# A PSUM bank moved, a merge step delayed and the samples' turns given their own steps, in the attention of a four-layer trunk

## The chip, the core and the metric

The kernel runs on one core of a Trainium2 chip. The metric is the device time of one execution in microseconds (us). A core has a matrix engine, TensorE (PE in the profile; its weight loads are PEld), which reads on-chip SBUF and writes the accumulator memory PSUM; three engines for elementwise work, VectorE (DVE), ScalarE (ACT) and GpSimd (POOL); and SyncE (SP), which here only issues DMA transfers. Each engine runs its own instructions in the order in which they were written, and waits on semaphores for the others. PSUM has eight banks. A bank that holds a result can be written again only when its readers are done.

## The reference, cut to what matters

A prompt of 1024 positions and 8 single-token samples go through an attention layer, a ConvGLU, a pooling layer and another ConvGLU. Only the attention is touched here. It has three groups of 16 heads, with dilations 1, 4 and 16; each query reads at most the 129 keys s-128..s of its own residue stream, and a bias table is added to the logits.

```python
    s = jnp.einsum("nbqhd,nbkhd->nbhqk", qb, kb).astype(jnp.float32) * SCALE
    s = s + bias[:, np.clip(rel, 0, SPAN)]
    s = jnp.where(valid[None, :, None], s, NEG_INF)
    m = jnp.max(s, axis=-1)
    p = jnp.exp(s - m[..., None])
    l = jnp.sum(p, axis=-1)
    o = jnp.einsum("nbhqk,nbkhd->nbqhd", p.astype(v.dtype), vb).astype(jnp.float32)
...
    w = l * jnp.exp(m - jnp.max(m, axis=0))
    w = w / jnp.sum(w, axis=0)
    return jnp.einsum("gbthd,gbth->bthd", o, w)
```

The last three lines merge the three groups per head. The samples do the same against caches of keys and values.

## The kernel before, in words

**Units.** The attention is cut into 24 units: eight pairs of heads (`hp`), each with the groups g = 2, 1, 0 in this order. For each unit TensorE makes q, k and v: nine groups of 24 matmuls (line 125; each float32 product is three fast products of high and low halves). While it does this for one unit, the attention of the unit before is fed in between the matmuls. A unit takes some 48 us.

**The order.** It is written by a plan, not by the hardware. `attend` lays down steps with a place on a clock that counts one for every three matmuls; a unit has 72 of them. For block i of 128 queries, `scores` stands at place 6i+1, the transposition of the softmax weights (`probs_t`, tile `pt`) at 6i+15 and the value sums (`pv`, tile `o`) at 6i+24; the transpositions of v (`transpose_v`, tile `vt`) stand at 4 and 28. `between()` runs what has come due. Two queues of small tasks hang on the same clock: `extra` takes one task at 4, 10, 16, ... and `behind` one at 7, 13, 19, .... What a task returns is put on `urgent`, of which one step is run after each three matmuls, ahead of the plan. What is left at the end of a unit is flushed.

**Packing.** The queries and keys of the next unit are split into high and low halves late in a unit: `pack_q` (lines 402 to 404) and `pack_k` (lines 413 to 415), between places 29 and 59, on DVE, ACT and POOL.

**Banks.** Matmuls of q, k, v have two banks (`mm`). The attention has six: three for `o`, one each for `pt`, `s` and `misc`. `misc` is shared by the transposed values `vt`, the merge's transposition `mt`, and all that the samples do: `qr`, `ssc`, `selfp`, the samples' value products `spv` (line 773) and their turned sums `spt` (line 796).

**Merge.** After g = 0 of a pair, `Merge` queues in `extra`: two pauses, `weights` (DVE lines 574 to 582, one exponential on ACT), `rows` (TensorE transposes the weights into `mt`, line 587; DVE copies them out, line 589; they go to DRAM), and then for each group a `fetch` of the weights spread over partitions and an `apply`, which multiplies and adds on POOL (lines 607 and 609), then `store`. With the places above, `weights` falls at place 64 and `rows` at 70 of a unit, the fetches and applies in the next unit.

**Samples.** Every odd pair also carries two heads' pairs of the samples (`Sample`, four in all, `pc` 0 to 3). Their value part, `values`, runs through twelve products; after each third one the sum is turned (`turn`: two tiny matmuls per head into `spt`, then two DVE adds, line 800).

Of the kernel before, what the change touches and what calls it, by code (L numbers as in the profile page):

```python
# [11 lines left out]
F32 = mybir.dt.float32  # L12
# [18 lines left out]
TAB = 384  # L31
# [16 lines left out]
def trunk(ctx: ExitStack, tc: tile.TileContext, a, out):  # L48
# [135 lines left out]
    class Norm:  # L184
        def __init__(self, x, gain, c, place, engines):


            self.engines = engines
            self.lows = [nc.vector] if gain == 3 else ([nc.vector, nc.gpsimd] * 2 + [nc.vector] * 4)[:8 if gain + c == 0 else 2]
            self.x, self.gain, self.c, self.place = x, gain, c, place  # L190
            self.c0, self.c1 = CHUNKS[c]
            self.w = self.c1 - self.c0
            self.blocks = sub_blocks(self.w)
            self.done, self.rows, self.acc, self.squares, self.pending = False, {}, [], 0, None
# [92 lines left out]
    with ExitStack() as ph:  # L287
        qp = ph.enter_context(tc.tile_pool(name="qkv", bufs=1))
        mmp = ph.enter_context(tc.tile_pool(name="mmp", bufs=1, space=PSUM))
        app = ph.enter_context(tc.tile_pool(name="app", bufs=1, space=PSUM))  # L290
# [8 lines left out]
        def load_x(c):  # L299
            c0, c1 = CHUNKS[c]  # L300
            for k in range(8):
                nc.sync.dma_start(out=xT[k][:, c0:c1], in_=a["x"][:, k, c0:c1])

        def place(kind, j=0, c=0):
            if kind in ("row", "square"):
                return qp.tile([128, 512], F32, name="nrow", tag="p", bufs=4)
            if kind == "acc":
                return part[:, j, CHUNKS[c][0]:CHUNKS[c][1]]
            if kind == "vec":
                return qp.tile([128, 4, 4], F32, name="nv", tag="nv", bufs=2)  # L310
            banks.rotate(1)
            return app.tile([128, 512], F32, name="nstat", tag=banks[0], bufs=3 if banks[0] == "o" else 1)

        nc.scalar.activation(warm, ones, AF.Sqrt)
        banks = deque(["o", "o", "pt", "misc", "o", "s"])
        load_x(0)
        w_load(0)
        nc.sync.dma_start(out=consts, in_=a["consts"])
# [14 lines left out]
        def tables():  # L333

            def step(g, tag, src):
                ps = app.tile([16, TAB], F32, name="btp", tag=tag)
                ps = ps[:, :src.stop - src.start]
                nc.tensor.matmul(ps, rb[:, 16 * g:16 * g + 16], onehots[g][:, src], start=True, stop=True)
                if src.start == 0:
                    nc.vector.scalar_tensor_tensor(masks[g], ps, -1.0, masks[g], op0=ALU.mult, op1=ALU.subtract)  # L340
                    nc.sync.dma_start(out=bias_tab[:, g], in_=masks[g])
                else:
                    bs = qp.tile([16, 512], F32, name="bs", tag="p", bufs=4)[:, :136]
                    nc.vector.tensor_copy(bs, ps)
                    nc.sync.dma_start(out=bias_smp[:, g], in_=bs)

            return [partial(step, g, *x) for g in (2, 1, 0) for x in (("s", slice(0, TAB)), ("pt", slice(TAB, TAB + 136)))]

        norms = [Norm(lambda k: xT[k], 0, c, place, (nc.vector, nc.gpsimd)) for c in range(3)]

        def squares(c):
# [74 lines left out]
        def has_prev(g, i):  # L426
            return (g == 0 and i > 0) or (g == 1 and i % 2 == 1)
# [47 lines left out]

        def probs_t(u, j):
            w = 256 if j < 7 and has_prev(u.g, j + 1) else 128
            ps = app.tile([128, 2, 256], F32, name="pt", tag="pt")
            for h in range(2):
                nc.tensor.transpose(ps[:, h, 0:128], u.p[j][:, h, 0:128], ident)  # L480
                if w == 256:
                    nc.tensor.transpose(ps[:, h, 128:256], u.p[j + 1][:, h, 128:256], ident)
            phl = qp.tile([128, 2, 2, 256], F32R, name="phl", tag="phl", bufs=2)
            nc.scalar.activation(phl[:, :, 0, :w], ps[:, :, :w], AF.Copy)  # L484
            nc.vector.tensor_sub(phl[:, :, 1, :w], ps[:, :, :w], phl[:, :, 0, :w].bitcast(F32))  # L485
            u.pt[j] = (phl, w)

        def pv_mm(u, j, b0, b1, first):


            q = (j + b0) % 2
            for h in range(2):
                for x in range(2):
                    nc.tensor.matmul(u.o[:, h, 128 * q:128 * (q + b1 - b0)], u.v[j // 4][:, j % 4, h, :],
                                     u.pt[j][0][:, h, x, 128 * b0:128 * b1], start=first and h + x == 0, stop=True,
                                     skip_group_check=True)

        def pv(u, j):
            first = j % 2 == 0
            if first:  # L500
                u.o = app.tile([128, 2, 256], F32, name="o", tag="o", bufs=3)
                if j and u.pt[j - 1][1] == 256:
                    pv_mm(u, j - 1, 1, 2, True)
                    first = False
            pv_mm(u, j, 0, 1 if j % 2 else u.pt[j][1] // 128, first)
            if j % 2:

                x = 256 * (j // 2 % 2)
                tmp = (part[:, 0, x:x + 256] if (u.hp, u.g) != order[23] else
                       qp.tile([128, 256], F32, name="ot", tag="ot", bufs=1))  # L510
                u.tmp = tmp, u.o
                for h, (own, other) in enumerate(((A, B), (B, A))):
                    nc.scalar.activation(tmp[own], u.o[other, h], AF.Copy)
# [35 lines left out]
        class Merge:  # L549
            def __init__(self, hp):  # L550
                self.hp, self.us = hp, [units[hp, g] for g in range(3)]
                self.st, self.cb = units[hp, 0].others, {}
                pause = lambda: None
                if hp < 7:
                    extra.extend([pause, pause, self.weights, self.rows])
                else:
                    self.weights()
                    extra.extend([pause, self.rows])
                if hp < 7:
                    extra.extend([lambda: self.fetch(2), pause, lambda: self.apply(2),  # L560
                                  lambda: self.fetch(1), lambda: self.apply(1),
                                  lambda: self.fetch(0), lambda: self.apply(0), pause, self.store])
                else:
                    extra.extend([lambda: [self.fetch(g) for g in (2, 1, 0)] and None, pause, lambda: self.apply(2),
                                  lambda: self.apply(1), lambda: self.apply(0), self.store])
# [56 lines left out]
        class Sample:  # L622
# [7 lines left out]
            def group(self, g):  # L630
# [21 lines left out]
                if g == 0:  # L652
# [11 lines left out]
                    for i in range(self.pc < 3, 13 + len(self.rooms)):  # L664
                        behind.append(lambda i=i: self.values(i))

            def cols(self, cache, g, b, n):
                row = cache[g][b][:, 256 * self.pc:256 * self.pc + 256]
                w = (128, 512, 2048)[g]
                return bass.AP(tensor=row.tensor, offset=row.offset,  # L670
                               ap=[[8 * w, 128], [1024 * w, n], [1, 256]])
# [81 lines left out]
            def values(self, n):  # L753


                todo = []
                m = n - len(self.rooms)
                if 0 <= m < 12:
                    i, g = divmod(m, 3)
                    if not g and i:  # L760
                        todo.append(partial(self.turn, i - 1, self.sum))
                    todo.append(partial(self.products, i, g, self.rooms[m % len(self.rooms)]))
                if m == 12:
                    todo.append(partial(self.turn, 3, self.sum))
                if n < 12:
                    todo.append(partial(self.fetch, n))
                return todo
# [34 lines left out]
        extra, behind = deque(), deque()  # L802
# [103 lines left out]
        for n, (hp, g) in enumerate(order):  # L906
            u = units[hp, g] = Unit()
# [8 lines left out]
            for i, (which, c) in enumerate(seq):  # L916
# [12 lines left out]
                ps = mmp.tile([128, 352], F32, name="mm", tag="mm", bufs=2)  # L929
# [58 lines left out]
        for n, ct in enumerate(OUT):  # L988
# [9 lines left out]
            for c in range(3):  # L998
                c0, c1 = CHUNKS[c]
                ps = mmp.tile([128, 352], F32, name="mm", tag="mm", bufs=2)  # L1000
# [51 lines left out]
    def norm(gain, c, *engines):  # L1052
        return Norm(lambda k: xT[k], gain, c, place, engines)
# [363 lines left out]
```

## Time and profile before

| what | us |
|---|---|
| median of 3 runs | 2878.77 (2878.76 to 2883.21) |
| the profiled execution | 2875.72 |
| its span, first to last instruction | 2873.9 |
| PE busy in the span | 2777.4 (97%) |
| DVE / ACT / POOL busy | 1629.4 / 1361.1 / 1074.2 |

The span is read in stretches. From 85 to 1160 us the units of the pairs 0 to 6 and most of 7 run; until 85 us the first norms and loads, from 1160 to 1400 us the end of the attention, the output projection and the first norms of the next layer; after that the ConvGLUs and the pooling layer. A matmul's row in the profile lasts about twice as long as the distance to the next one, since they are pipelined: "busy" hides part of a wait, and what counts is when the next one starts.

### The profile page before, as it was taken

The page shows a single profiled execution, that of the slowest core. Times are in us where ns is not written, and L with a number is a line of the kernel's source. Part 1 is how long each engine was busy: PE and PEld are TensorE (multiplying, and loading weights), DVE is VectorE, ACT ScalarE, POOL GpSimd, SP SyncE. Part 2 cuts the span into 40 slices and gives each one's busy share as a digit, 9 for nine tenths or more (in the row PEclk, how much of TensorE's full clock was granted, in tenths as well). Part 3 has the DMA queues.
Part 4 walks back from the last instruction along what each step waited for, and adds up shares of the span by engine and source line. Part 5 has one row for each costly group of instructions (what it writes and reads, how often), then busy time and mean ns, then how long its engine had stood idle before and what let it go on. Part 6 is the DMA issues. An engine that isn't in the chain of part 4 may idle for free. (4 is left out here: it accounts for less than half of the span.)

```text
span 2873.9 us, 46685 instructions
## 1 busy us (share of the span) xinstructions
PE 2777.4 (97%) x18109; PEld 2736.4 (95%) x18109; DVE 1629.4 (57%) x3330; ACT 1361.1 (47%) x2748; POOL 1074.2 (37%) x865
## 2 busy tenths in 40 slices
PE   6999999999999999999999999999999999999998
PEld 5999999999999998899999999999999999999998
DVE  6666656665666566755333234687755334346655
ACT  5565665566556665634223223445542233334443
POOL 4335453545354535445444434111133343331110
PEclk9999999999999999999999999999999999999999
DMA  3234332433243333537222222333422226223543
GB/s 115 61 76 135 85 98 74 124 96 96 79 120 99 93 81 108 169 111 99 74 67 74 67 74 74 110 118 118 135 88 67 74 67 76 73 68 116 173 143 92
DMA packets 203949, 277.80 MB, mean 97 GB/s; under 512 B 70272, under 2 KB 154096, under 8 KB 203728
## 3 DMA queue, kind: packets, MB, share of 16 engines
q1 hardware_dynamic: 203680, 274.80, 34.8%
q8 instruction: 142, 2.33, 0.3%
q14 instruction: 79, 0.65, 0.1%
q10 hardware_dynamic: 48, 0.02, 0.0%
HBM read 251.89 MB, written 23.34 MB: 96 GB/s over the span
## 5 line engine op out<-in xcount | busy, mean ns | idle before, releaser
L125 PE MATMUL mm<-hh,w_hi 128*128 128x352 f32 (+2 forms) x4064 | 1340.5, 330 | 9.3 <-ACT hh L256 3.3
L125 PE MATMUL mm<-hl,w_hi 128*128 128x352 f32 (+2 forms) x4064 | 1305.3, 321 | 5.0 <-DVE hl L260 5.0
L125 PE MATMUL mm<-hh,w_lo 128*128 128x352 f32 (+2 forms) x4064 | 1305.2, 321 | 1.8 <-DVE w_lo L105 1.8
L125 PEld LDWEIGHTS mm<-hh,w_hi 128*128 128x128 f32 x4064 | 769.8, 189 | 15.7 <-ACT hh L256 3.8
L125 PEld LDWEIGHTS mm<-hl,w_hi 128*128 128x128 f32 x4064 | 770.5, 190 | 7.1 <-DVE hl L260 6.5
L125 PEld LDWEIGHTS mm<-hh,w_lo 128*128 128x128 f32 x4064 | 768.9, 189 | 2.6 <-DVE w_lo L105 2.6
L105 POOL TENSOR_TENSOR w_lo<-w_raw,w_hi 128x1024 fp32r<-128x1024 f32 x212 | 514.0, 2425 | 574.2 <-ACT w_hi L104 561.3
L104 ACT ACTIVATE w_hi<-w_raw 128x1024 fp32r<-128x1024 f32 x348 | 364.7, 1050 | 290.7 <-PE mm L125 266.0
L1119 DVE SCALAR_TENSOR_TENSOR conv<-gate,convp,conv 128x336 f32<-128x336 f32 (+1 forms) x176 | 220.5, 1253 | 384.9 <-ACT conv L1117 375.9
L125 PE MATMUL mm<-gh,w_hi 128*128 128x352 f32 (+2 forms) x1056 | 340.5, 322 | 4.0 <-ACT gh L1110 2.1
L125 PE MATMUL mm<-gh,w_lo 128*128 128x352 f32 (+2 forms) x1056 | 339.9, 322 | 1.9 <-DVE w_lo L105 1.9
L125 PE MATMUL mm<-gl,w_hi 128*128 128x352 f32 (+2 forms) x1056 | 339.8, 322 | 0.3 <-POOL gl L1111 0.3
L1057 DVE TENSOR_TENSOR x<-x,mm 128x352 f32<-128x352 f32 (+2 forms) x312 | 157.1, 510 | 225.8 <-PE mm L125 225.3
L472 ACT ACTIVATE p<-p,st 128x128 f32<-128x128 f32 (+1 forms) x384 | 169.9, 443 | 201.4 <-DVE st L469 200.7
L1111 POOL TENSOR_TENSOR gl<-conv,gh 128x352 fp32r<-128x352 f32 (+2 forms) x132 | 123.5, 937 | 339.1 <-ACT gh L1110 336.1
L105 DVE TENSOR_TENSOR w_lo<-w_raw,w_hi 128x1024 fp32r<-128x1024 f32 x136 | 166.7, 1226 | 87.6 <-ACT w_hi L104 87.5
L125 PEld LDWEIGHTS mm<-gh,w_hi 128*128 128x128 f32 x1056 | 199.8, 189 | 4.6 <-ACT gh L1110 2.4
L125 PEld LDWEIGHTS mm<-gh,w_lo 128*128 128x128 f32 x1056 | 200.1, 190 | 2.2 <-DVE w_lo L105 2.2
L125 PEld LDWEIGHTS mm<-gl,w_hi 128*128 128x128 f32 x1056 | 199.9, 189 | 0.7 <-POOL gl L1111 0.7
L485 DVE TENSOR_TENSOR phl<-pt,phl 128x512 fp32r<-128x512 f32 (+1 forms) x192 | 104.7, 545 | 167.0 <-ACT phl L484 165.9
L373 ACT ACTIVATE raw<-mm 128x336 f32<-128x336 f32 (+1 forms) x216 | 144.5, 670 | 99.1 <-PE mm L125 96.7
L1102 ACT ACTIVATE gate<-mm 128x352 f32<-128x352 f32 (+2 forms) x132 | 60.2, 457 | 262.1 <-PE mm L125 262.1
(190 smaller groups left out, 3118.6 us busy)
## 6 DMA issues: line engine op xcount, KB each, us to landing
w_raw<-in_w_in SPq DMA_DIRECT2D x176, 512.0 KB
w_raw<-in_w_out SPq DMA_DIRECT2D x88, 512.0 KB
w_raw<-in_w_qkv SPq DMA_DIRECT2D x72, 512.0 KB
x<-qd SPq DMA_DIRECT2D x48, 256.0 KB
kc<-in_cache_k SPq DMA_DIRECT2D x48, 256.0 KB
vc<-in_cache_v SPq DMA_DIRECT2D x48, 256.0 KB
x<-c_d SPq DMA_DIRECT2D x42, 256.0 KB
out_new_k<-raw SPq DMA_DIRECT2D x8, 516.0 KB
```

What stands on the lines that cost most here:

```text
L104: nc.scalar.activation(hi, raw, AF.Copy)
L105: (eng or (nc.vector if i in quick else nc.gpsimd)).tensor_sub(lo, raw, hi.bitcast(F32))
L125: nc.tensor.matmul(ps, l, r, start=first and i == 0, stop=last and i == n - 1)
L373: nc.scalar.activation(stream(raw[:, :T], u.g, c0, t1, which > 0), ps[:, :w].rearrange("p (s r) -> p s r", r=DILS[u.g]), AF.Copy, scale=si ...
L472: nc.scalar.activation(p[:, h, :w], p[:, h, :w], AF.Exp, bias=u.st[:, i, h, 0:1], scale=-1.0, accum_out=u.st[:, i, h, 1:2])
L485: nc.vector.tensor_sub(phl[:, :, 1, :w], ps[:, :, :w], phl[:, :, 0, :w].bitcast(F32))
L1057: nc.vector.tensor_add(xT[ct][:, c0:c1], xT[ct][:, c0:c1], ps)
L1102: nc.scalar.activation(gate[:, 2 + s:2 + e], group(tiles8(w, c), c), AF.Copy)
L1111: nc.gpsimd.tensor_sub(self.gl[f][:, s:e], conv[:, s:e], self.gh[f][:, s:e].bitcast(F32))
L1119: nc.vector.scalar_tensor_tensor(conv[:, :n], gate[:, j:j + n], cw[j], conv[:, :n], op0=ALU.mult, op1=ALU.add)
```

## The change: what it does

Three edits. One of the three banks of `o` becomes a second bank of `pt` (the norms' and the bias table's temporary tiles follow suit). In the merges of the pairs 0 to 6 a pause is put between `weights` and `rows`: `rows` and all that follows in the merge come one `extra` place (six clock places) later. For the samples 0 to 2 `turn` is no longer returned by `values` along with a product, but is a task of its own in `behind`, so that the later products each come one to four places later; sample 3 stays as it was.

```diff
             banks.rotate(1)
-            return app.tile([128, 512], F32, name="nstat", tag=banks[0], bufs=3 if banks[0] == "o" else 1)
+            return app.tile([128, 512], F32, name="nstat", tag=banks[0], bufs=2 if banks[0] in ("o", "pt") else 1)
...
-        banks = deque(["o", "o", "pt", "misc", "o", "s"])
+        banks = deque(["o", "o", "pt", "misc", "pt", "s"])
...
-                ps = app.tile([16, TAB], F32, name="btp", tag=tag)
+                ps = app.tile([16, TAB], F32, name="btp", tag=tag, bufs=2 if tag == "pt" else 1)
...
-            ps = app.tile([128, 2, 256], F32, name="pt", tag="pt")
+            ps = app.tile([128, 2, 256], F32, name="pt", tag="pt", bufs=2)
...
-                u.o = app.tile([128, 2, 256], F32, name="o", tag="o", bufs=3)
+                u.o = app.tile([128, 2, 256], F32, name="o", tag="o", bufs=2)
...
                 if hp < 7:
-                    extra.extend([pause, pause, self.weights, self.rows])
+                    extra.extend([pause, pause, self.weights, pause, self.rows])
...
                     for i in range(self.pc < 3, 13 + len(self.rooms)):
                         behind.append(lambda i=i: self.values(i))
 
+                        if self.pc < 3 and i and i % 3 == 0:
+                            behind.append(lambda i=i: self.turn(i // 3 - 1, self.sum))
+
...
-                    if not g and i:
+                    if not g and i and self.pc == 3:
                         todo.append(partial(self.turn, i - 1, self.sum))
                     todo.append(partial(self.products, i, g, self.rooms[m % len(self.rooms)]))
-                if m == 12:
+                if m == 12 and self.pc == 3:
                     todo.append(partial(self.turn, 3, self.sum))
```

TensorE's order at the start of the unit after the merge of pair 0, as a difference (`mt` is the merge's transposition, `vt` the transposed values; both live in the one bank `misc`):

```order
 L125 MATMUL mm<-hh,w_lo 128x352
 L445 MATMUL vt<-consts,raw 128x128 x4
+L587 MATMUL mt<-consts,me 48x128
 L125 MATMUL mm<-hh,w_hi 128x352
 L125 MATMUL mm<-hl,w_hi 128x352
```

`mt` stood three matmuls ahead of the unit's end and now stands right behind the four transpositions into `vt`, with no matmul between them. The same holds at all seven merges of the pairs 0 to 6.

TensorE's order at the first turn of sample 0, as a difference (`spt` is the turned sum, `spv` the samples' product; both in `misc`):

```order
-L125 MATMUL mm<-hh,w_lo 128x336
-L796 MATMUL spt<-selm,spv_sb 128x4 x2
-L125 MATMUL mm<-hh,w_hi 128x336
-L125 MATMUL mm<-hl,w_hi 128x336
-L125 MATMUL mm<-hh,w_lo 128x336
-L773 MATMUL spv<-x_3561,pst 16x256 x4
+L799 MATMUL spt<-selm,spv_sb 128x4 x2
+L125 MATMUL mm<-hh,w_hi 128x336
+L125 MATMUL mm<-hl,w_hi 128x336
+L125 MATMUL mm<-hh,w_lo 128x336
```

Three matmuls stood between the turned sum and the next product in the same bank; now the product comes a whole `behind` place later. (Line numbers behind the new lines are three higher.)

GpSimd's order in the second unit after the merge of pair 0, before:

```order
L105 TENSOR_TENSOR w_lo<-w_raw,w_hi 128x1024
L607 TENSOR_TENSOR x_1403<-x_1403,x_2369 128x1024
L609 TENSOR_TENSOR x_916<-x_916,x_1403 128x1024
L404 TENSOR_TENSOR x_593<-raw,x_593 64x512
L650 TENSOR_TENSOR kc<-kc,x_2377 128x512
L607 TENSOR_TENSOR x_1913<-x_1913,x_2488 128x1024
L609 TENSOR_TENSOR x_916<-x_916,x_1913 128x1024
L650 TENSOR_TENSOR kc<-kc,x_2377 128x512
L404 TENSOR_TENSOR x_593<-raw,x_593 64x512
L105 TENSOR_TENSOR w_lo<-w_raw,w_hi 128x1024
L650 TENSOR_TENSOR kc<-kc,x_2377 128x512
L415 TENSOR_TENSOR k_100<-raw,k_100 64x512
```

and after (607 and 609 are the merge's multiply and add, 404 and 415 pack queries and keys, 650 multiplies the samples' keys, 105 splits weights):

```order
L105 TENSOR_TENSOR w_lo<-w_raw,w_hi 128x1024
L404 TENSOR_TENSOR x_593<-raw,x_593 64x512
L607 TENSOR_TENSOR x_1403<-x_1403,x_2430 128x1024
L609 TENSOR_TENSOR x_916<-x_916,x_1403 128x1024
L650 TENSOR_TENSOR kc<-kc,x_2374 128x512 x2
L404 TENSOR_TENSOR x_593<-raw,x_593 64x512
L607 TENSOR_TENSOR x_1913<-x_1913,x_2532 128x1024
L609 TENSOR_TENSOR x_916<-x_916,x_1913 128x1024
L105 TENSOR_TENSOR w_lo<-w_raw,w_hi 128x1024
L650 TENSOR_TENSOR kc<-kc,x_2374 128x512
L415 TENSOR_TENSOR k_100<-raw,k_100 64x512
```

The last multiply and add of the merge stood ahead of the second part of the queries; now they stand behind it, where the keys are packed.

## Rows read from the trace of the kernel before

**Rows 1.** Windows: stretch and length; each engine's busy us; PE clock; DMA.
```profile
85.00:1160.00 1075.00, 1038.79 (x7143) 1016.12 (x7142) 693.05 (x1802) 643.06 (x1629) 483.20 (x285) 1.00 0.36 97
```
**Rows 2.** Waits of PE, 85 to 1160 us: total us, times, longest.
```profile
PE pt L480 <- DVE phl L485: 11.7, 15, 1.7
PE o L494 <- DVE phl L485: 9.2, 9, 1.9
PE mt L587 <- DVE me L582: 8.7, 4, 2.2
PE spv L773 <- DVE so L800: 5.4, 6, 1.3
PE spt L796 <- DVE ct L589: 1.0, 3, 0.3
```
**Rows 3.** Timeline at an odd pair's merge: start, us, instruction [idle before, releaser].
```profile
347.98 0.91 PE L773 MATMUL spv<-x,pst 128*16 128x256 f32 x4 [1.26 <-DVE so L800]
...
359.84 0.60 PE L796 MATMUL spt<-selm,spv_sb 16*128 16x4 f32 x4 [0.32 <-DVE ct L589]
361.00 0.62 PE L773 MATMUL spv<-x,pst 128*16 128x256 f32 x4 [0.55 <-DVE so L800]
...
364.47 0.41 PE L125 MATMUL mm<-hh,w_hi 128*128 128x352 f32 x1
365.38 0.69 DVE L449 TENSOR_TENSOR vhl<-vt,vhl 128x512 fp32r<-128x512 f32 x1 [1.55 <-ACT vhl L448]
```
**Rows 4.** Windows of 3.3 us around two of the samples' waits.
```profile
348.20:351.50 3.30, 3.30 (x15) 3.12 (x13) 1.97 (x4) 1.26 (x2) 2.09 (x3) 0.50 0.68 236
352.00:355.30 3.30, 3.30 (x25) 3.17 (x25) 2.42 (x7) 1.74 (x3) 0.38 (x1) 1.00 0.23 67
...
928.50:931.80 3.30, 3.30 (x15) 3.17 (x14) 1.98 (x4) 1.26 (x2) 2.16 (x3) 0.50 0.70 234
```
**Rows 5.** Timeline at an even pair's merge and into the next unit.
```profile
201.36 0.44 PE L480 MATMUL pt<-consts,p 128*128 128x128 f32 x2 [0.48 <-DVE phl L485]
...
207.54 0.55 PE L494 MATMUL o<-phl,vhl 128*128 128x128 f32 x3 [0.58 <-DVE phl L485]
...
212.21 0.29 PE L587 MATMUL mt<-consts,me 128*48 128x128 f32 x1 [2.18 <-DVE me L582]
212.72 0.85 DVE L530 TENSOR_TENSOR x<-o,part 64x256 f32<-64x256 f32 x2
213.60 0.28 DVE L589 COPY ct<-mt 48x128 f32<-48x128 f32 x1
214.11 1.06 ACT L104 ACTIVATE w_hi<-w_raw 128x1024 fp32r<-128x1024 f32 x1
215.82 0.40 PE L125 MATMUL mm<-hh,w_hi 128*128 128x352 f32 x1
216.73 0.69 DVE L449 TENSOR_TENSOR vhl<-vt,vhl 128x512 fp32r<-128x512 f32 x1 [1.55 <-ACT vhl L448]
```
**Rows 6.** Timeline of PE, DVE and POOL in that next unit, packing stage.
```profile
237.57 0.44 PE L480 MATMUL pt<-consts,p 128*128 128x128 f32 x2 [0.84 <-DVE phl L485]
...
241.78 2.41 POOL L607 TENSOR_TENSOR x<-x,x 128x1024 f32<-128x1024 f32 x1 [3.58 <-DMA x<-c_d]
244.27 2.51 POOL L609 TENSOR_TENSOR x<-x,x 128x1024 f32<-128x1024 f32 x1
244.51 2.82 DVE L404 TENSOR_TENSOR x<-raw,x 64x512 fp32r<-64x512 f32 x1
249.16 0.44 PE L480 MATMUL pt<-consts,p 128*128 128x128 f32 x2 [0.57 <-DVE phl L485]
256.21 0.55 PE L494 MATMUL o<-phl,vhl 128*128 128x128 f32 x3 [1.91 <-DVE phl L485]
```
**Rows 7.** One line's durations, 85 to 1160 us: ns min/median/max, start, form.
```profile
L404 DVE TENSOR_TENSOR x<-raw,x x45: 686/687/2894, 97.5 to 1152.5; 64x512 fp32r<-64x512 f32 x45
L607 POOL TENSOR_TENSOR x<-x,x x21: 2382/2395/2412, 220.5 to 1111.3; 128x1024 f32<-128x1024 f32 x21
```

## The prediction

> **What bounds the kernel now.** First the windows by stage: between 85 and 1160 us, where the change lies, TensorE shows 1038.8 of 1075 us busy at the full clock, so about 36 us of idle time is all that three edits to the order of the attention can remove there [rows 1]. DVE is busy 693 us in the same stretch: on average it is far from full. Then TensorE's waits in this stretch [rows 2]. They add up to 36.0 us, and every one of them ends with a DVE instruction. That is the thing to see: the three edits aim at four of the five rows (pt, mt, spv, spt: 26.8 us), but what is late each time is DVE. Where DVE is late because its own queue is full, a wait that is taken away from one place comes back at the next thing that TensorE needs from DVE. So I read the timeline at each wait and asked whether DVE stands idle soon after it (then the wait is really saved) or works without a pause until the next wait (then it is given back).
>
> **The samples' turns.** The turned sum and the next product share the bank misc, with three matmuls between them; now a whole place lies between. The six spv waits (5.4 us) and the three spt waits behind the merge's copy (1.0 us) go, and DVE has idle time there: it waits 1.55 us for ACT at 365 us [rows 2, 3]. That is -6.4 us. The long one of these waits also costs something after it: behind the waits at 348 and 928 us the granted clock is 0.50, the lower of the two levels, 1.2 GHz, and 15 matmuls start in 3.3 us where 25 start at the full clock [rows 4]. One such stretch costs 3.3 x 10 / 25 = 1.3 us; two go: -2.6 us.
>
> **The pause, at the odd pairs' merges (three: 1, 3, 5).** The pause puts mt directly behind the four transpositions into vt, in the same single bank. mt can be written only when ACT and DVE have read vt, and all matmuls stand behind mt in TensorE's queue. Before, TensorE went on at 364.47 us, and DVE's read of vt ended at 365.38 + 0.69 = 366.07 [rows 3]. The new wait is 1.6 us; there was no mt wait at these merges (the four that there are belong to the even pairs). Bounds: 0.7 us (DVE's subtraction alone, with ACT's copy already done) and 2.2 us (the longest mt wait in rows 2). I take 1.6, since both ends of it are read here: 3 x 1.6 = +4.8 us.
>
> **The pause, at the even pairs' merges (four: 0, 2, 4, 6).** Here mt waited 2.18 us for the weights, and the pause does remove that. But the unit before is the one with DVE full: from the pt wait at 201.36 over the o wait at 207.54 to the merge's weights, DVE hardly stops [rows 5]. What comes then in DVE's queue before vt is read is unchanged: the adds that end at 213.57, the evacuations, the first scores, with ACT's split of weights (to 215.17) and two exponentials between, then the subtraction from vt, which ended at 217.42. Only the merge's copy (0.28 us) leaves that queue. So the bank comes free at about 217.1 us, whether TensorE stands before it 2.2 us earlier or not. Before, TensorE went on behind vt at 215.82 us. The balance is 217.1 - 215.8 = +1.3 us for each, and it already contains the 2.18 us saved and the two small waits ahead of it (0.48 of pt, 0.58 of o), which are swallowed: 4 x 1.3 = +5.2 us. Bounds: if ACT and DVE did move forward with TensorE, the wait would be the 1.6 us of the odd pairs against 2.18 + 0.48 + 0.58 saved, -1.6 us each; if they don't move at all, 217.42 - 215.82 = +1.6 us. I take +1.3, near the end that the row of the subtraction gives.
>
> **The second bank of pt.** Fifteen waits, 11.7 us, 0.8 us each [rows 2]: four in each even pair's two units' time around a merge at the places of 201, 237 and 249 us (twelve in all), and three in the units after the odd merges. With two banks a transposition needs DVE's read of the one before last, so these waits go as such. What is late next is o: the value sums need the low halves that the same DVE subtraction writes. At 237.57 us (0.84 us) DVE has slack soon after: 4 x 0.84 = -3.4 us. For the three others I take the mean: 3 x 0.8 = -2.3 us. The places of 201 and 249 us are given back: the first to the merge (above), the second to the o wait at 256.21, since DVE packs queries and keys from 244 to 256 us without a pause and its last subtraction for o is at the end of that [rows 6]. Zero for these eight; if they were saved too, 11.7 - 3.4 - 2.3 = 6.0 us more.
>
> **One bank less for o.** Zero: none of the waits in rows 2 is for a bank of o, and an o bank is asked for again only after another one has been filled, 12 places on. If that cover went, the wait would be the add that empties it, up to 0.85 us [rows 5]; below zero nothing, since a bank taken away frees nothing.
>
> **What is moved: the applies.** The pause moves three multiplies and two adds of 2.4 us each on POOL by a place, and the order shows where the last pair ends up: it stood before the second part of the queries, now it stands behind it, in front of the weights' split, where DVE packs. That matters, as POOL's instructions hold up DVE's: a DVE subtraction of 64x512 takes 0.69 us in the median and up to 2.89 [rows 7]; the one that started at 244.51, just behind POOL's add of 244.27 to 246.78, ended at 247.33, 2.1 us late [rows 6]. From 241.78 us on POOL has work in both orders; after, its longest two (before at 241.78 and 244.27, the first beside DVE work that reads PSUM) run later, beside the packing. Bounds for the o wait behind the packing: a gain of 2.1 us (that one hold-up gone by luck of the phase) and a loss of 2.4 us (one more whole multiply in front of a DVE instruction). No row decides; I take half a multiply, 1.2 us at the four even pairs: +4.8 us. SP's transfers move along (the weights' fetches stand behind the queries' rows of the samples, the weight loads in front of them); TensorE never waits for a DMA or a weight half in this stretch [rows 2], so zero there, and up to the 0.3 to 1.3 us of a sample's product where POOL's multiply now stands before its value split.
>
> **New low-clock stretches.** Two waits with 1.3 us of idle time each were followed by 3.3 us at a clock of 0.50 [rows 4]. The mean from 85 to 1160 us rounds to 1.00, so it lost under 0.005 x 1075 = 5.4 us of full clock, which is three such stretches at most (0.5 x 3.3 each): nearly all mt and o waits of 2 us left the clock alone [rows 1, 2]. Whether the seven new waits at vt and the four longer o waits do it can't be read. Bounds: none and all eleven, 0 to 14.3 us. I take three: +3.9 us.
>
> **Sum.** -6.4 - 2.6 + 4.8 + 5.2 - 3.4 - 2.3 + 4.8 + 3.9 = +4.0 us. The profiled execution took 2875.72 us (span 2873.9, 1.8 us around it), so it would take 2879.7; it lies 3.05 us below the median of the runs shown, 2878.77, and the same +4.0 us on that median gives 2882.8: 2883 us.
>
> **Rivals.** *The waits really go.* If DVE's lateness at the merge and in the packing is a matter of phase and not of a full queue, pt gives 11.7, the even merges -1.6 each (-6.4, of which 4 x 0.48 is already in pt: -4.5), the turns 6.4 + 2.6, the odd merges cost 4.8, nothing for applies and clock: -20.4 us, 2858 us. For it: DVE's 64% busy share [rows 1]. Against it: in the stretches of rows 5 and 6 the waits follow each other. Chance 0.27.
>
> *The applies block the packing, and the clock falls with it: slower.* The mechanism is DVE's packing beside POOL's multiply and add. It decides from the point at which one more 2.4 us instruction stands before a DVE instruction that the o wait depends on: +2.4 us at four places instead of 1.2 (+4.8), and then TensorE stands for 4 us and more, and at seven instead of three places the low clock follows (+5.2): 4.0 + 10.0 = +14.0 us, 2893 us. For it speaks the 2.82 us row; against it that POOL was already busy there, so that one hold-up may only replace another. The Trainium skill, "SBUF — State Buffer", section "Who interferes with whom", has a rule by which this would be the outcome: of a GpSimd instruction and a DVE instruction with two SBUF inputs the one that issues first keeps the shared port pair for its whole length, and the other does not run slower but stands still. The row at 244.51 agrees (it ended 0.55 us behind POOL's add). Chance 0.28.
>
> The forecast has 0.45, with 2874 to 2891 as its own range. That an edit does nothing is in it: the pause, which frees mt of the weights but puts it behind vt.
>
> **The numbers.** 0.2% of the median, 5.8 us, is about what a measurement of this kernel can tell from no change: 2873 to 2884.5. Of the forecast's 0.45 I put 0.02 below, 0.25 within, 0.18 above; of the fast rival 0.25 below and 0.02 within; of the slow one 0.02 within and 0.26 above: 0.27, 0.29, 0.44. The range reaches to 2857 (some 0.13 of the fast rival lies below) and 2898 (0.05 above).
>
> **What would show it.** Right: no wait spv <- so and none of mt for the weights; seven waits of mt for DVE line 449, 1.5 us at odd and over 3 us at even merges; pt waits gone or nearly; o waits grown from 9.2 us to 15 or more. Wrong: mt waits under 1 us at the even merges (ACT and DVE moved forward with TensorE), or o waits no longer than before (the packing isn't full), which would make it the fast rival. DVE's longest rows of lines 404, 413 and 415 beside lines 607 and 609 tell whether the applies block.

## The result: slower, by far more than forecast

The changed kernel took 2913.7 us (median of 6 runs, 2906.4 to 2921.0), the kernel before 2879.8 us (6 runs). The ratio is 1.0119, 95% interval 1.0106 to 1.0132: 33.9 us slower. The forecast of 2883 us had the direction; the size lies outside its range.

### The profile after

The profiled execution took 2911.06 us, 35.3 us more than the one of before. The windows show in which way. Columns as in [rows 1]; the stretch is 40 us longer, since about the same work (7170 matmuls against 7143) ends later.

```profile
85.00:1200.00 1115.00, 1060.39 (x7170) 1037.38 (x7169) 712.45 (x1809) 646.29 (x1633) 487.55 (x287) 0.98 0.34 94
```

TensorE is idle for 1115.00 - 1060.39 = 54.6 us, against 36.2 us [rows 1]: 18.4 us of the loss. And its mean clock in this stretch is 0.98 where it was 1.00. The waits, as in [rows 2], from 85 to 1200 us:

```profile
PE o L494 <- DVE phl L485: 26.2, 17, 4.7
PE mt L587 <- DVE vhl L449: 17.8, 7, 3.4
PE spv L776 <- POOL x L794: 4.6, 6, 1.1
PE spv L776 <- ACT x L793: 2.2, 3, 0.7
PE spt L799 <- DVE spv_sb L781: 1.4, 3, 1.0
```

All that the three edits aimed at is gone: no wait of pt, none of mt for the weights, none of a sample's product for `so`. In their place stand seven mt waits for the read of vt, o waits of 26.2 us, and a new kind: the samples' products and their turns wait 8.2 us for ACT, POOL and DVE. The granted clock, in windows of 3.3 us as in [rows 4], behind the first even merge and behind the o wait of the packing stage:

```profile
216.80:220.10 3.30, 3.30 (x14) 3.30 (x13) 0.59 (x2) 0.71 (x1) 0.03 (x1) 0.50 0.49 123
259.50:262.80 3.30, 3.30 (x12) 3.30 (x13) 3.25 (x5) 0.76 (x2) 2.01 (x2) 0.50 0.32 130
261.10:264.40 3.30, 3.30 (x13) 3.30 (x13) 3.27 (x7) 0.08 (x1) 0.41 (x1) 0.50 0.02 5
265.00:268.30 3.30, 3.30 (x25) 3.28 (x24) 1.10 (x6) 3.01 (x8) 1.20 (x1) 1.00 0.30 83
```

At a clock of 0.50 (1.2 GHz) 12 to 14 matmuls start where 25 do at 1.00 (2.4 GHz): 1.5 to 1.7 us lost for each such length (3.3 x 11 / 25 to 3.3 x 13 / 25), and less where TensorE waits for a part of it. From 85 to 1200 us the records show 14 of them, at nine places (at five places two in a row): six behind the even merges, six behind waits of the packing stages, two in the units behind the odd merges, and none behind the 1.41 us waits of mt at the odd merges. The kernel before had two up to 1160 us [rows 4]. What the idle time leaves of the loss is 35.3 - 18.4 = 16.9 us, which would be twelve more lengths at 1.4 us; this share of the clock is what is left over, it was not measured by itself.

The even merge, as in [rows 5]:

```profile
212.20 0.85 DVE L530 TENSOR_TENSOR x<-o,part 64x256 f32<-64x256 f32 x2
...
215.08 0.57 ACT L448 ACTIVATE vhl<-vt 128x512 fp32r<-128x512 f32 x1
...
215.69 0.69 DVE L449 TENSOR_TENSOR vhl<-vt,vhl 128x512 fp32r<-128x512 f32 x1 [1.44 <-ACT vhl L448]
216.44 0.29 PE L587 MATMUL mt<-consts,me 128*48 128x128 f32 x1 [3.39 <-DVE vhl L449]
```

mt stands 3.39 us before a bank that DVE frees at 216.38. Here the working was right: the waits of this stretch are now 1.30 (o) + 3.39 us against 0.48 + 0.58 + 2.18 us [rows 5], which is +1.45 us; +1.3 was forecast.

The packing stage, as in [rows 6]:

```profile
248.03 2.64 POOL L607 TENSOR_TENSOR x<-x,x 128x1024 f32<-128x1024 f32 x1 [0.17 <-POOL x L404]
249.09 1.87 DVE L413 CAST k<-raw 64x512 fp32r<-64x512 f32 x1
250.75 2.46 POOL L609 TENSOR_TENSOR x<-x,x 128x1024 f32<-128x1024 f32 x1
...
251.32 2.17 DVE L413 CAST k<-raw 64x512 fp32r<-64x512 f32 x1
253.17 2.56 POOL L105 TENSOR_TENSOR w_lo<-w_raw,w_hi 128x1024 fp32r<-128x1024 f32 x1
253.53 2.75 DVE L415 TENSOR_TENSOR k<-raw,k 64x512 fp32r<-64x512 f32 x1
...
258.99 0.42 DVE L485 TENSOR_TENSOR phl<-pt,phl 128x256 fp32r<-128x256 f32 x1
259.47 0.90 PE L494 MATMUL o<-phl,vhl 128*128 128x128 f32 x3 [4.67 <-DVE phl L485]
```

POOL's multiply, add and weight split stand one behind the other, and DVE's instructions beside them last 1.87 to 2.75 us, each ending just behind one of POOL's. The Trainium skill, "SBUF — State Buffer", section "Who interferes with whom", calls this a port pair that one of the two engines keeps for a whole instruction; the 2.75 us row agrees (it ended 0.55 us behind POOL's). TensorE then stands 4.67 us once, where before it stood 0.84, 0.57 and 1.91 us [rows 6]. Over the four packing stages the waits are 15.9 us now and 14.5 before: +1.4 us, as the forecast's terms for this place give (-3.4 + 4.8). The idle time is as forecast; that most of it comes in one piece (4.7, 3.5 and 4.2 us at three of the four stages) is not.

Last, the unit behind an odd merge, where before there was one pt wait of 0.5 to 0.6 us:

```profile
390.82 2.45 POOL L609 TENSOR_TENSOR x<-x,x 128x1024 f32<-128x1024 f32 x1
391.06 2.76 DVE L404 TENSOR_TENSOR x<-raw,x 64x512 fp32r<-64x512 f32 x1
393.85 0.42 DVE L485 TENSOR_TENSOR phl<-pt,phl 128x256 fp32r<-128x256 f32 x1
394.33 0.55 PE L494 MATMUL o<-phl,vhl 128*128 128x128 f32 x3 [0.61 <-DVE phl L485]
...
396.97 0.29 PE L776 MATMUL spv<-x,pst 128*16 128x256 f32 x1 [0.73 <-ACT x L793]
396.99 1.27 POOL L794 TENSOR_TENSOR x<-vc,x 128x512 fp32r<-128x512 f32 x1 [3.72 <-ACT x L793]
398.31 0.53 PE L776 MATMUL spv<-x,pst 128*16 128x256 f32 x3 [1.06 <-POOL x L794]
```

DVE's subtraction is held up by POOL's add; the softmax row and the evacuations behind it come late to ACT, ACT's split of a sample's values with them, then POOL's half of it, then the product. With the o waits later in the unit (2.1 us in the first and the third, 0.5 us in the second), TensorE waits 4.7, 3.6 and 4.5 us in the three units of this kind, 12.8 us against 1.6.

How much time that costs can be read from ACT's reads of vt (line 448), which come in the same order in both kernels. Round an odd merge, from the second read in the unit that holds it to the first read two units on, before:

```profile
324.56 0.60 ACT L448 ACTIVATE vhl<-vt 128x512 fp32r<-128x512 f32 x1 [0.32 <-PE vt L445]
411.42 0.60 ACT L448 ACTIVATE vhl<-vt 128x512 fp32r<-128x512 f32 x1
```

and after:

```profile
330.76 0.60 ACT L448 ACTIVATE vhl<-vt 128x512 fp32r<-128x512 f32 x1 [0.32 <-PE vt L445]
422.41 0.60 ACT L448 ACTIVATE vhl<-vt 128x512 fp32r<-128x512 f32 x1
```

That is 86.86 us before and 91.65 after, +4.8 us; it is +5.4 and +3.2 us at the other two, +13.4 us in all. The last part of it, behind the merge, lasts 8.0, 7.1 and 6.4 us longer, and the part before is shorter, as some of the samples' products have moved from one to the other.

### The profile page after: what moved, and what is told of

Read it like the earlier page. It is cut to its first block, busy times and chain, and to the rows that moved or that the text cites. A ratio compares the mean times of both kernels' runs of the same rounds, so it can differ in the third digit from the quotient of the medians.

```text
span 2909.3 us, 46675 instructions
## 1 busy us (share of the span) xinstructions
PE 2795.0 (96%) x18109; PEld 2753.8 (95%) x18109; DVE 1645.6 (57%) x3330; ACT 1361.5 (47%) x2748; POOL 1074.9 (37%) x865
## 5 line engine op out<-in xcount | busy, mean ns | idle before, releaser
L125 PEld LDWEIGHTS mm<-hh,w_hi 128*128 128x128 f32 x4064 | 776.0, 191 | 14.6 <-ACT hh L256 3.8
```

Of the source, the lines that this page charges most:

```text
L125: nc.tensor.matmul(ps, l, r, start=first and i == 0, stop=last and i == n - 1)
```

## The experiments

Every kernel is given with its own median and that of the kernel before on the same chip. The edits are against the kernel before unless it is said otherwise. Where two experiments are compared, the difference is that of their medians; taken from their ratios to the kernel before, it differs by up to 2 us.

**Each edit alone.** The bank edit (`pt` with two banks, `o` with two):

```
-            ps = app.tile([128, 2, 256], F32, name="pt", tag="pt")
+            ps = app.tile([128, 2, 256], F32, name="pt", tag="pt", bufs=2)
-                u.o = app.tile([128, 2, 256], F32, name="o", tag="o", bufs=3)
+                u.o = app.tile([128, 2, 256], F32, name="o", tag="o", bufs=2)
```

> The bank edit alone. Theory A (DVE's full queue and the low clock make the loss, the bank is innocent): the 15 pt waits of 11.7 us go, some 6 us of them come back as o waits for line 485 (9.2 to about 15 us), no wait for an o bank appears, and the time falls by 3 to 7 us to 2873 to 2877. Rival B (the third o bank was needed: the o waits rose from 9.2 to 26.2 us because of it): o waits of 20 us or more here too, and a time of 2885 or more.

The pause:

```
-                    extra.extend([pause, pause, self.weights, self.rows])
+                    extra.extend([pause, pause, self.weights, pause, self.rows])
```

> The pause alone. Theory A: it carries most of the 34 us: mt waits for line 449 of some 3.4 us at the four even and 1.4 us at the three odd merges, the applies run beside the packing and lengthen the o or pt waits at 256 us and its like by 2 to 3 us, and the low clock follows the long ones: 2893 to 2903 us. If the pause costs only the mt waits less the 8.7 us removed, 2888 us. Rival C (the samples' turns carry the loss): within 5 us of before.

The turns (a queued step of their own for each):

```
+                        if self.pc < 3 and i and i % 3 == 0:
+                            behind.append(lambda i=i: self.turn(i // 3 - 1, self.sum))
-                    if not g and i:
+                    if not g and i and self.pc == 3:
```

> The turns in steps of their own, alone. Theory A: the waits of spv for so (5.4 us) go and with them two low-clock stretches (2.6 us), -8 us; the later products meet the applies of the unit after, where the applies stand as before, so that the new spv waits for POOL and ACT (6.8 us with all three edits) are half as long or less: 2873 to 2880 us. Rival C: the later products are themselves the loss in the second unit after an odd merge (6 to 7 us at each of three): 2886 to 2895 us, with spv waits for line 791 of 4 us or more and a longer o wait there.

Measured: the bank edit 2887.8 us (before 2878.2; ratio 1.0029, 1.0019 to 1.0040), the pause 2909.3 us (1.0101, 1.0083 to 1.0119), the turns 2887.8 us (1.0026, 1.0014 to 1.0039). None of the three is worth anything by itself, and the pause costs most, 6 us more than the upper end of what was expected of it. The bank edit and the turns came out in the ranges of their rivals (B and C). With the bank edit alone the waits read:

```profile
PE o L494 <- DVE phl L485: 28.3, 13, 4.7
PE spv L773 <- DVE so L800: 5.4, 6, 1.3
```

pt's waits are gone, and the time has moved into o; the two together have grown from 22.4 us (both to 1200 us) to 28.3. They end with the low halves (line 485), so the reason that rival B gave isn't seen: no wait for a bank of o is there. With the turns alone the waits for `so` are gone, and those for POOL's split are there:

```profile
PE spv L776 <- POOL x L794: 7.5, 6, 2.1
PE spv L776 <- DVE ct L589: 1.2, 3, 0.4
```

**All three edits, with mt in a bank of o** (against the changed kernel):

```
-                ps = app.tile([48, 128], F32, name="mt", tag="misc")
+                ps = app.tile([48, 128], F32, name="mt", tag="o", bufs=2)
```

> All three edits, with the merge's transposed weights in a bank of o in place of misc. It takes the seven waits of mt for line 449 away (17.8 us) and the low clock behind some of them. If a wait taken away here is really saved: 2885 to 2892 us. If DVE's queue is full at the even merges (theory A), the next thing that TensorE needs there is late instead (the second scores or the second vt), and only the odd ones (4.2 us) and the clock are saved: 2898 to 2907 us. A wait of mt for an o bank (line 530) would show that o's two banks are too few.

Measured: 2885.4 us (ratio 1.0025, 1.0014 to 1.0036), 28 us less than the changed kernel, by one word. The mt waits (17.8 us) are gone and come back as 2.4 us only:

```profile
PE o L494 <- DVE phl L485: 28.6, 16, 4.7
PE spv L776 <- POOL x L794: 4.6, 6, 1.1
PE spv L776 <- ACT x L793: 2.2, 3, 0.7
```

So the clash of mt and vt in `misc` costs 28 us against the same three edits without it: 15.4 us of waits; the other 13 us are what is left. The low clock has a part in them: from 85 to 1200 us the records show nine lengths of it here and 14 with the clash.

**Is it the clock?** The bank edit alone, with 14 matmuls that nobody reads put into its long o waits (one in each of the four packing stages behind an even merge):

```
+                    if h + x == 0 and j == 7 and u.g == 2 and u.hp % 2:
+                        fill = app.tile([128, 512], F32, name="fill", tag="s")
+                        for n in range(14):
+                            nc.tensor.matmul(fill, hh[:, 0, 0:128], hh[:, 0, 0:512], start=True, stop=True)
```

> The bank edit alone, with 14 idle matmuls of 128x512 (into the free bank of the scores, read by nobody) between the first and the second value-sum matmul of block 7 in the four units where the bank edit alone showed a 4.7 us o wait with 6.8 us at half clock behind it. They add about 3 us of TensorE work inside each wait. Theory A (what the bank edit costs is the low clock behind one long wait in place of several short ones): the four stretches of 6.8 us vanish, 4 x 2.5 to 3.4 us comes back, and the time goes from 2887.8 to 2877 to 2881 us. Theory B (the idle time itself counts, the clock is a side show): no gain, 2887 to 2892 us, since work was added.

Measured: 2877.7 us (before 2880.1; ratio 0.9990, 0.9981 to 0.9998), 10.1 us less than the bank edit alone, with more work done. The windows of the first packing stage, without and with the added matmuls:

```profile
235.00:270.00 35.00, 30.39 (x194) 30.11 (x193) 26.20 (x51) 17.36 (x42) 20.94 (x12) 0.90 0.51 133
```

```profile
235.00:270.00 35.00, 34.68 (x229) 33.66 (x228) 28.11 (x58) 19.31 (x49) 24.42 (x14) 1.00 0.57 154
```

The clock stays at 1.00 and 21 more matmuls fit beside the 14. Theory A holds against B, since added work makes the kernel faster: the low clock behind one long wait is a large part of what the bank edit costs. How much of the gain is the clock and how much the wait, which shrinks too, the runs don't separate.

**The pause without its clash.** The pause alone, mt in a bank of o (three banks):

> The pause alone, with mt in a bank of o instead of misc. The pause alone took 2909.3 us (+31). Theory A: the clash of mt and vt in the one bank misc is what the pause costs: the mt waits (17.3 us) and the low clock behind them go, and what is left is the applies beside the packing (pt and o waits of 11.7 and 9.2 us grown to 19.5 and 14.8 us): 2881 to 2890 us. Theory B (the pause's later steps on POOL are what costs): 2900 us or more. The forecast's own reading at the even merges (a saved wait is given back, since DVE's queue is full): no mt wait, but o or pt waits behind it longer by about 2 us at each of the four, 2895 us or more.

and the same with POOL's and SP's work in the order of before, which separates mt's place from the moved applies:

```
-                    extra.extend([pause, pause, self.weights, pause, self.rows])
+                    extra.extend([pause, pause, self.weights, pause])
-                    extra.extend([lambda: self.fetch(2), pause, lambda: self.apply(2),
+                    extra.extend([lambda: [self.rows(), self.fetch(2)] and None, pause, lambda: self.apply(2),
```

> The pause with mt in a bank of o, but the samples' fetches and applies in the order of the kernel before: against the pause with mt in a bank of o alone (2885.6 us) it differs in POOL's and SP's order and nothing else. Theory A (moving the applies beside the packing costs more than the 4.8 us of the forecast): 2876 to 2880 us, and o waits back from 18.4 us to about 11. Theory B (the place of the applies matters little, what costs is the mt wait given back): 2883 us or more, with o and pt waits as they were (18.4 and 15.1 us).

Measured: 2885.6 us (ratio 1.0019, 1.0010 to 1.0028) and 2876.9 us (0.9984, 0.9974 to 0.9994). The order of the applies alone is worth 8.7 us, as theory A of the second expectation has it. DVE's packing of the keys with the applies moved (line, operation, tiles, count | busy us, mean ns | idle before):

```profile
L413 DVE CAST k<-raw 64x512 fp32r<-64x512 f32 x92 | 112.4, 1222 | 2.1
L415 DVE TENSOR_TENSOR k<-raw,k 64x512 fp32r<-64x512 f32 x46 | 62.0, 1347 | 1.6
```

and its waits for the low halves:

```profile
PE o L494 <- DVE phl L485: 18.4, 13, 4.1
PE pt L480 <- DVE phl L485: 15.1, 13, 2.3
```

The same with the applies in their old order, first the packing:

```profile
L413 DVE CAST k<-raw 64x512 fp32r<-64x512 f32 x92 | 105.6, 1148 | 2.1
L415 DVE TENSOR_TENSOR k<-raw,k 64x512 fp32r<-64x512 f32 x46 | 55.7, 1211 | 1.6
```

then the waits:

```profile
PE pt L480 <- DVE phl L485: 14.6, 13, 3.1
PE o L494 <- DVE phl L485: 10.3, 8, 2.8
```

With the applies moved, these 138 instructions on the keys take 13.1 us longer in all (the queries' two lines 5.0 us less), and the o waits are 8.1 us longer. (The profiled execution of the second kernel lies 8.6 us below its median, so its trace is read for order and waits, not for the clock.) The longer waits are not where the forecast put them. In the unit behind the first odd merge (366 to 417 us) TensorE waits, with the applies moved:

```profile
PE pt L480 <- DVE phl L485: 3.3, 2, 1.9
PE o L494 <- DVE phl L485: 0.9, 1, 0.9
```

and with the applies in their old order:

```profile
PE pt L480 <- DVE phl L485: 0.6, 1, 0.6
```

In the three units of this kind these waits are 11.3 us against 1.8; at the four packing stages behind the even merges, 14.7 us against 17.2. By these waits the moved applies cost what they cost behind the odd merges, and not at the four stages for which the forecast priced them. And the pause itself, freed of both, gains 2.6 us by the medians where it removes 8.7 us of mt waits: pt's waits have grown from 11.7 to 14.6 us, those of `so` from 5.4 to 6.6.

**The turned sum in a bank of o**, the order of the steps unchanged:

```
-                ps = app.tile([128, 2, 2, 2], F32, name="spt", tag="misc")
+                ps = app.tile([128, 2, 2, 2], F32, name="spt", tag="o", bufs=3)
```

> The kernel before with the turned sum of a sample in a bank of o, the order of the steps unchanged. Theory A (turns of their own were right in what they remove, and lost it by putting later products beside the applies): the spv waits for so (5.4 us), the spt waits (1.0 us) and the two low-clock stretches at 348 and 928 us go and nothing comes back: -6 to -9 us, 2870 to 2873 us. Theory B (what is saved there is given back at the next wait for DVE or POOL, whatever the order): within 3 us of before.

Measured: 2870.7 us (ratio 0.9964, 0.9951 to 0.9977), 9.4 us faster. Of the 6.4 us of waits in [rows 2] this is left:

```profile
PE spv L773 <- POOL x L791: 0.5, 3, 0.2
```

The turns' saving is real; steps of their own lose it by making the later products late.

The stretch round an odd merge, read by line 448 as above in the profiled executions, sets these side by side (sum of the three, against the kernel before):

| kernel | us |
|---|---|
| turned sum in a bank of o | -9.2 |
| the turns alone | +5.2 |
| pause, mt in a bank of o, applies in their old order | -3.1 |
| pause, mt in a bank of o | +11.0 |
| the pause alone | +17.3 |
| all three edits | +13.4 |

Either the moved products or the moved applies are enough to lose some 12 to 14 us here, and the two losses don't add up when both edits are made. (Some of each number is chance of the clock: a low length is 1.5 us or so.)

**Both in banks of o** (this and the last two edits of mt together, POOL's order as before):

> The kernel before with the turned sum and mt in banks of o, and with mt one place behind the merge's weights, but the samples' fetches and applies left in the order they have in the kernel before. Theory A (the three waits that the change aims at can be removed without the clash in misc and without moving POOL's work): -6 to -9 us for the turns and another 4 x 1.5 to 2.2 us for the mt waits, 2861 to 2868 us. Theory B (the waits come back behind DVE's full queue at the even merges): as with the turned sum alone, 2870 to 2880 us, with o or pt waits that have grown by the 8 us.

Measured: 2868.3 us (ratio 0.9957, 0.9945 to 0.9970), 2.4 us less than with the turned sum alone, a difference inside the intervals. The time lies between the two theories; the waits say B.

```profile
PE pt L480 <- DVE phl L485: 17.2, 15, 2.8
PE o L494 <- DVE phl L485: 10.7, 9, 1.9
```

The mt waits (8.7 us) are gone, and pt's have grown from 11.7 to 17.2 us: most of it is given back, though not at the merge. At the four merges the waits of pt, o and mt fall from 13.2 to 3.8 us; at the four packing stages those of pt and o grow from 14.5 to 20.5 us.

**The bank edit on top**, without and with the 14 idle matmuls:

> The version with mt and the turned sum in banks of o (2868.3 us), with the change's bank edit on top (two banks of pt, two of o). Theory A (the second bank of pt merges short waits into one long wait for the low halves, with the low clock behind it, also where nothing else is changed): pt waits of 17.2 us gone, o waits up from 10.7 to 25 us or more, low-clock stretches of 6.8 us at the packing, 2872 to 2878 us. Theory B (the bank edit only failed for company's sake): 2855 to 2864 us.

> The same with the bank edit, and with the 14 idle matmuls of 128x512 in the long o wait of the four even units. Theory A (idle time can be had for nothing there, the clock is what costs): back under the version without the bank edit, 2860 to 2867 us. Theory B: 2868 us or more, the 12 us of added work are paid for.

Measured: 2873.0 us (ratio 0.9968, 0.9956 to 0.9980) and 2861.8 us (0.9934, 0.9922 to 0.9947). Without them, the one row of waits for the low halves and the window of the stretch:

```profile
PE o L494 <- DVE phl L485: 25.4, 16, 3.5
```

```profile
85.00:1200.00 1115.00, 1085.47 (x7414) 1064.43 (x7413) 734.65 (x1890) 676.34 (x1706) 507.93 (x305) 0.99 0.36 99
```

and the same two with them:

```profile
PE o L494 <- DVE phl L485: 10.8, 13, 1.6
```

```profile
85.00:1200.00 1115.00, 1097.85 (x7522) 1073.06 (x7521) 739.42 (x1905) 678.82 (x1718) 512.23 (x306) 1.00 0.36 100
```

The waits of pt and o together fall from 27.9 to 25.4 us with the second bank of pt, and yet the time doesn't fall (ratio 0.9968 against 0.9957 without it, intervals that overlap). With the waits filled it falls by 11.2 us, to where the intervals no longer touch. This is the fastest version of all: 17.7 us faster than before, 51.9 us faster than the change.

**A short fill.** Six idle matmuls at the same place, one bank of pt:

> The version with mt and the turned sum in banks of o, with six idle matmuls (1.3 us) between the first and the second value-sum matmul of block 7 in the four even units, where it waited 1.2 to 1.9 us. Theory A (the clock): the four stretches of 3.4 us at half clock at 256, 543, 812 and 1119 us go where the wait at this place is the cause, up to 4 x 1.4 = -5.6 us, 2863 to 2868 us. Theory B (those stretches belong to the pt waits of 1.8 to 2.9 us some 20 us earlier, or to no single wait): within 2 us of 2868 us, or later by up to 4 x 1.3 us.

Measured: 2868.9 us (ratio 0.9953, 0.9940 to 0.9965), as without them, so by the median theory B holds: where the wait is split over pt and o, filling the o part gains nothing that can be measured. But the profiled execution, the fastest of the five (2864.3 us, the others 2868.8 to 2870.5), shows a clock of 1.00 at all four places, as theory A says. Whether the low clock stays there in the others isn't shown.

## Why the prediction was wrong

By places, with the forecast's terms and the distances between reads of line 448 in the two profiled executions. (An even merge is read from the second read in its unit to the second in the next, the packing stage from there to the third read after it.)

| place | forecast | measured |
|---|---|---|
| three odd merges with the unit behind | -6.4 - 2.6 + 4.8 - 2.3 = -6.5 | +13.4 |
| four even merges with the half unit ahead | +5.2 | +13.2 |
| four packing stages behind them | -3.4 + 4.8 = +1.4 | +10.5 |
| new low clock, no place given | +3.9 | in the three above |
| the rest | 0 | -1.8 |

**The unit behind an odd merge: taken as a gain of 2.3 us, it is where most of the forecast's error lies.** None of the prediction's timeline rows is from there. The waits for `so` went as worked out, the term -6.4, and the turned sum in another bank shows that they can be had (-9.4 us with the clock). But two steps failed. The forecast took for granted that what comes behind a turn stays where it is; turns of their own push the later products further into the next unit, beside the applies. And it priced the moved applies at the four even pairs only and put nothing for them behind the odd merges; for a sample's product behind POOL's multiply it named a price ("up to the 0.3 to 1.3 us of a sample's product") and took zero. Measured in those three units: 6.8 us of new waits for ACT's and POOL's splits and for the sum, and o waits of 6.0 us. That is +11.2 us of idle time, most of what the forecast missed in idle time (+18.4 us against the +2.7 of its terms without the clock). Each of the two does it alone: the moved products in the turns alone, the moved applies in the pause with mt in a bank of o.

**New low-clock stretches: the term +3.9 was mis-sized.** Three were taken of a bound of eleven, at 1.3 us; there were 14, and the two old ones went: by what the idle time leaves, +16.9 us net, against the forecast's +3.9 - 2.6. The reason for choosing three, that most waits of 2 us had left the clock alone in the kernel before, doesn't carry over to waits of 3.4 and 4.7 us. And the bank edit was costed by the sum of the waits, where what counts is also whether they come as one. The added matmuls show it: -10.1 us on the bank edit alone, -11.2 us on the best order.

**The merges were right in idle time.** Odd merges: 1.41 us each (1.6 forecast). Even merges: +1.45 us at the first (1.3); what they cost beyond that goes with the six lengths of low clock behind them. That mt's saved wait is given back for the most part holds in two experiments (2.6 us had of 8.7, and 2.4 us), but not for the forecast's reason: without the clash it is saved at the merge and lost in the packing stage. When mt waits for the bank instead, another bank saves nearly all of it (15.4 of 17.8 us).

**The second bank of pt and the applies** came out as the sum says in idle time at the four packing stages (+1.4 us), but by luck: neither part is right. The bank edit alone takes the waits there from 14.5 to 19.7 us, where -3.4 was forecast, and the moved applies alone don't lengthen them (14.7 us against 17.2), where +4.8 was taken. **One bank less for o** shows no cost, as forecast: no run shows a wait for a bank of o. It was not tried apart from the second bank of pt.

The signs that the forecast named for being right (no wait for `so`, seven waits of mt for line 449, pt's waits gone, o's above 15 us) all came. None of them concerns the units behind the odd merges or the clock, so they could not tell a loss of 4 us from one of 34.

The slow rival ("the applies block the packing, and the clock falls with it") named the packing beside the applies and the clock behind it, and stopped at seven lengths of low clock; it, too, lacked the units behind the odd merges.

## What to carry to other kernels

Before a step is given a place of its own, list everything behind it that moves too, and look at what that then stands beside: here the products and the applies that nobody meant to move cost more than the waits that were removed. Do so for every kind of unit in which the step occurs, not for one of them. Count not only how long the bound engine will wait but in how few pieces: several short waits merged into one can cost as much as they did apart or more, even where their sum is no longer, and work that nobody reads may pay for itself there. Where two tiles share a bank, try another bank before another order.

## What was not expected of the hardware

A wait filled with 3.4 us of matmuls without a reader made the kernel 10 to 11 us faster over four places. Nor does one length of idle time set the clock: the 1.26 us before 348 us was followed by a clock of 0.50 [rows 3, 4], while the kernel before shows 1.00 on the mean with nine o waits of up to 1.9 us [rows 1, 2]. And kernels of one order spread more than expected: the order with the old applies lay between 2868.4 and 2880.3 us in 12 executions. Their granted clock goes with it: 0.991 or 0.992 on the mean in the four shortest, 0.988 or 0.989 in the four longest. What makes the clock differ was not tried.
